# A gated MLP's down projection as two-by-two block products with seven multiplications

## The chip, the core and the metric

One core of a Trainium2 chip runs the whole program. The metric is device time in microseconds for one launch. Engines are named as in the profile: PE (TensorE matmul), PEld (its weight loads), DVE (VectorE), ACT (ScalarE), POOL (GpSimd), SP (SyncE, which issues the loads).

## The reference

Two decoder layers work on x of 256 tokens by 2048 features, in float32. Each layer adds a mixer's output to x (layer 0: gated spatial mixing and a gated linear recurrence; layer 1: attention) and then that of a gated MLP. The change is in the MLP alone:

```python
def conv_ffn(h, w_up, conv_w, conv_b, w_down):
    seq = h.shape[1]
    z = h @ w_up                                   # 2048 -> 2 x 5632
    zp = jnp.pad(z, ((0, 0), (CONV_WIDTH - 1, 0), (0, 0)))
    z = sum(conv_w[j] * zp[:, j:j + seq] for j in range(CONV_WIDTH)) + conv_b
    a, b = jnp.split(z, 2, axis=-1)
    return (jax.nn.silu(a) * b) @ w_down           # 5632 -> 2048
...
        h = rms_norm(x, ffn_norm[l])
        x = x + conv_ffn(h, ffn_w_up[l], ffn_conv_w[l], ffn_conv_b[l], ffn_w_down[l])
```

## The kernel before

**Layout.** Features lie on the 128 partitions, tokens on the free axis. x is 16 tiles xT[m] of 128 features by 256 tokens. The 5632 hidden features are 44 tiles (HT), the up projection has 88 blocks: 44 for a, 44 for b.

**Three products for one.** Every float32 matrix product is made of faster matmuls on a rounded part and its remainder. For a weight chunk w, `weights` loads it from SP's queue (L137), ACT copies it into wh with rounding (L139), and DVE computes the remainder wl = w - wh (L141). The activations were split in the same way (`split`, L200 and L201), with both parts side by side in one tile of 512 columns. `project` then runs, for each tile of 128 input features, one matmul of wh with all 512 columns (L155) and one of wl with the 256 rounded columns (L157), accumulating in one PSUM bank. This pair is the unit of work in both projections. A later operation adds the bank's two halves.

**Buffers.** The pool wp has four buffers for w and three each for wh and wl. Inside the MLP a second pool (fw, kept in `deep`) adds four w, two wh and two wl, and every other chunk goes there. PSUM has three banks pm for projections and five others for the rest, in pools that live for the whole program.

**Order inside the MLP.** The program text gives the order, and a static scheduler settles how each engine's stream interleaves; every engine then works its stream in order. The hidden tiles are worked in four groups of eleven (GRP). `up(g)` makes 22 up blocks: `conv` is a projection over 16 feature tiles in two chunks of eight (16 pairs), the addition of the halves (L187, L188), the norm's factor R (L195) and the width-3 convolution (L673 on ACT, L674 and L675 on DVE); for each a and b there follow Silu on ACT, the product (L685) and the split into a tile hid. `down(g)` projects a group's eleven hidden tiles on each of the 16 output tiles m (chunks of 6 and 5 tiles, 11 pairs) and `add_x` adds the result to xT[m]: ACT copies one half out of PSUM (L264), DVE adds the other and then the copy (L265, L266). The order is up(0), up(1), down(0), up(2), down(1), up(3), down(2), down(3). In layer 0 the last `down` also feeds the next norm: a split of xT[m] (L203, L204) and its square (L239, L240). In layer 1 it stores xT[m] instead (L696).

Of the kernel before, what the change touches and what calls it, by code (L numbers as in the profile page):

```python
# [19 lines left out]
CH = 16  # L20
HID = 5632
HT = HID // P
GRP = 11
EPS = 1e-6
WARM = 12
LEVELS = (64, 32, 16, 8, 4, 2, 1)
# [18 lines left out]
def tile_trunk(ctx: ExitStack, tc: tile.TileContext, x, pp_d, cst_d, mlev_d, msk_d,  # L45
# [8 lines left out]
    pm = ctx.enter_context(tc.tile_pool(name="pm", bufs=3, space=bass.MemoryType.PSUM))  # L54
    px = ctx.enter_context(tc.tile_pool(name="px", bufs=1, space=bass.MemoryType.PSUM))

    count = [0]

    def nm(base):
        count[0] += 1  # L60
        return f"{base}_{count[0]}"
# [36 lines left out]
    def back(ap):  # L98
        return view(ap, P - 1, (-1, P))

    def bank(tag="px"):
        n = nm(tag)
        return px.tile([P, 512], F32, tag=tag, name=n, bufs=banks[tag])

    banks = {"px": 5}
    flight, queue = [], []

    def tick():
# [11 lines left out]
    warm = pm.tile([P, 512], F32, tag="pm", name="warm")  # L120
    for i in range(WARM):
        PE.matmul(warm[:, 0:P], ones, ones, start=True, stop=True)

    def drain():
        while flight or queue:
            tick()

    deep = {"pool": None, "turn": 0}

    def weights(src, n):  # L130
        deep["turn"] += 1
        if deep["pool"] is not None and deep["turn"] > 6 and deep["turn"] % 2:
            pool, nw, ns = deep["pool"], 4, 2
        else:
            pool, nw, ns = wp, 4, 3
        w = pool.tile([P, n], F32, tag="w", name=nm("w"), bufs=nw)
        nc.sync.dma_start(w, src)  # L137
        wh = pool.tile([P, n], F32R, tag="wh", name=nm("wh"), bufs=ns)
        SC.activation(wh, w, AF.Copy)  # L139
        wl = pool.tile([P, n], F32R, tag="wl", name=nm("wl"), bufs=ns)  # L140
        V.tensor_tensor(wl, w, wh.bitcast(F32), ALU.subtract)  # L141
        return wh, wl

    def project(wsrc, acts, chunks=(8, 8), k0=0):
        ps = pm.tile([P, 512], F32, tag="pm", name=nm("pm"))
        nk = sum(chunks)
        done = 0
        for c in chunks:
            lo = (k0 + done) * P
            tick()  # L150
            wh, wl = weights(wsrc[:, lo:lo + c * P], c * P)
            for k in range(c):
                a = acts[done + k]
                first, last = done + k == 0, done + k == nk - 1
                PE.matmul(ps, wh[:, k * P:(k + 1) * P], a,  # L155
                          start=first, stop=False, skip_group_check=True)
                PE.matmul(ps[:, S:2 * S], wl[:, k * P:(k + 1) * P], a[:, 0:S],  # L157
                          start=False, stop=last, skip_group_check=True)
            done += c
        return ps  # L160

    def project_tok(wsrc, norm, feed=False):
        ps = [pm.tile([P, 512], F32, tag="pm", name=nm("pm")) for _ in range(2)]
# [58 lines left out]
    class Norm:  # L222
# [21 lines left out]
            self.feed_split(k)  # L244
            self.feed_square(k)

        def finish(self, tok=False):
            ps = bank()
# [12 lines left out]

    def add_x(m, ps):
        t = tp.tile([P, S], F32, tag="ev", name=nm("ev"), bufs=3)
        SC.activation(t, ps[:, S:2 * S], AF.Copy)  # L264
        V.tensor_tensor(xT[m], xT[m], ps[:, 0:S], ALU.add)  # L265
        V.tensor_tensor(xT[m], xT[m], t, ALU.add)  # L266

# [1 line left out]
    def mixer_ab(norm):  # L269
        es = ExitStack()  # L270
        hp = es.enter_context(tc.tile_pool(name="hp", bufs=1))

        def quad(n):
            return hp.tile([P, 512], F32R, tag="two", name=nm(n), bufs=2 * NH)
# [258 lines left out]
        es.close()  # L533
        return nxt

# [1 line left out]
    def mixer_c(norm):  # L537
        es = ExitStack()
        hp = es.enter_context(tc.tile_pool(name="cpool", bufs=1))
        dp = es.enter_context(tc.tile_pool(name="dp", bufs=1, space=bass.MemoryType.DRAM))  # L540
        A = norm.a
        R, Rt = norm.finish(tok=True)
# [109 lines left out]
        es.close()  # L652
        return nxt

# [1 line left out]
    def ffn(l, norm, last):  # L656
        es = ExitStack()
        hp = es.enter_context(tc.tile_pool(name="fp", bufs=1))
        deep.update(pool=es.enter_context(tc.tile_pool(name="fw", bufs=1)), turn=0)
        A = norm.a  # L660
        R = norm.finish()
        nxt = None if last else Norm(C_MIX + KT)

        def conv(j):
            z = project_norm(w_up[l, j], A, R)
# [12 lines left out]
        def up(g):  # L678
            hid = []
            for i in range(GRP):  # L680
                j = g * GRP + i
                a = conv(j)
                b = conv(HT + j)
                act(a, a, AF.Silu)
                V.tensor_tensor(a, a, b, ALU.mult)  # L685
                t = hp.tile([P, 512], F32R, tag="hid", name=nm("hid"), bufs=2 * GRP)
                split(t, a)
                hid.append(t)
            return hid

        def down(g, hid):
            for m in range(KT):
                add_x(m, project(w_dn[l, m], hid, chunks=(6, 5), k0=g * GRP))
                if g == HT // GRP - 1:
                    if last:
                        nc.sync.dma_start(out[:, m, :], xT[m])  # L696
                    else:
                        nxt.feed(m)

        hids = [up(0)]  # L700
        for g in range(HT // GRP):
            if g + 1 < HT // GRP:
                hids.append(up(g + 1))
            down(g, hids[g])
        deep["pool"] = None
        es.close()
        return nxt

    banks.update(px=3, pd=2)
    norm = mixer_ab(Norm(C_MIX))  # L710
    norm = ffn(0, norm, False)
    norm = mixer_c(norm)
# [81 lines left out]
```

## Time and profile before

| | |
|---|---|
| time, median of 3 runs | 2391.18 us (2377.88 to 2404.29) |
| span of the profiled execution, first to last instruction | 2389.0 us (the page gives no other time for it) |
| PE, PEld | 2377.3 us (100%), 2060.0 us (86%) |
| DVE | 1756.3 us (74%) |
| ACT | 1317.2 us (55%) |
| POOL | 16.1 us (1%) |
| DMA packets | 440.73 MB, mean 184 GB/s |

Rows of groups read: line, engine, operation, tiles, shapes and count, then the busy time in us and the mean ns of one, then the idle time just before them and what ended it. Busy time is the time covered, so overlapping instructions of a group count once. Rows of waits read: who waited for whom, us in total, times, the longest. Rows of stretches read: start and end, length, then busy us and instructions of each engine, the granted clock, the share of the DMA engines' time and GB/s.

### The profile page before, as it was taken

What the parts mean: (1) busy time and instruction counts of PE and PEld (TensorE: products, weight loads), DVE (VectorE), ACT (ScalarE), POOL (GpSimd) and SP (SyncE); (2) the same over time, 40 slices, a digit from 0 to 9 for tenths busy, and PEclk for the clock granted to TensorE, in tenths of its full rate; (3) what the DMA queues carried; (4) which work ended last, traced back from release to release, by engine and by line L of the source; (5) the groups of instructions that cost most, each with busy time, mean ns of one, the idle gap of its engine ahead of it and who ended that gap; (6) DMA issues with size and microseconds to landing.
All of it is one profiled execution on the core that took longest, in us unless ns stands there. A gap on an engine that the chain in (4) does not pass through costs nothing.

```text
span 2389.0 us, 35728 instructions
## 1 busy us (share of the span) xinstructions
PE 2377.3 (100%) x13198; PEld 2060.0 (86%) x13198; DVE 1756.3 (74%) x2954; ACT 1317.2 (55%) x2169; POOL 16.1 (1%) x20
## 2 busy tenths in 40 slices
PE   8999999999999999999999999999999999999999
PEld 7888888888888888888888888888888888888888
DVE  6767786888867877777756666777777767767765
ACT  6655565655555555555545455556555555545543
POOL 2000000000000000000000000000000000000000
PEclk9999999999999999999999999999999999999999
DMA  7544455755566566566655555557555565565564
GB/s 265 177 159 135 141 184 187 241 190 191 169 187 213 177 173 222 176 170 188 200 175 177 175 159 167 188 192 237 186 186 186 156 220 186 152 220 185 153 188 145
DMA packets 133869, 440.73 MB, mean 184 GB/s; under 512 B 14880, under 2 KB 16944, under 8 KB 133440
## 3 DMA queue, kind: packets, MB, share of 16 engines
q1 hardware_dynamic: 132224, 433.40, 57.5%
q10 hardware_dynamic: 1440, 5.01, 0.6%
q8 instruction: 104, 1.70, 0.3%
q14 instruction: 69, 0.57, 0.1%
q0 software_dynamic: 32, 0.05, 0.0%
HBM read 436.29 MB, written 2.11 MB: 184 GB/s over the span
## 4 chain that ended last, share of the span: by engine, by line
PE 97%; DMA 1%; DVE 1%; issue 0%; ACT 0%; SPq 0%; DVEq 0%; ACTq 0%
PE pm L155 53%; PE pm L157 27%; PE pm L177 5%; PE pm L178 5%; PE pm L176 5%; PE px L439 1%; DVE wl L141 0%; DMA w<-in_w_v 0%; DMA mst<-in_mlev 0%; PE pd L411 0%; DMA w<-in_w_up 0%; PE pd L412 0%; PE px L612 0%; PE px L576 0%; PE px L583 0%
## 5 line engine op out<-in xcount | busy, mean ns | idle before, releaser
L141 DVE TENSOR_TENSOR wl<-w,wh 128x1024 fp32r<-128x1024 f32 (+3 forms) x900 | 1015.7, 1129 | 538.1 <-ACT wh L139 534.3
L139 ACT ACTIVATE wh<-w 128x1024 fp32r<-128x1024 f32 (+3 forms) x900 | 883.4, 982 | 952.2 <-PE pm L155 653.4
L155 PE MATMUL pm<-a,wh 128*128 128x512 f32 x3600 | 1266.0, 396 | 0.0
L157 PE MATMUL pm<-a,wl 128*128 128x256 f32 x3600 | 1010.5, 281 | 0.5 <-DVE wl L141 0.5
L155 PEld LDWEIGHTS pm<-a,wh 128*128 128x128 f32 x3600 | 675.0, 187 | 157.1 <-DVE a L204 0.8
L157 PEld LDWEIGHTS pm<-a,wl 128*128 128x128 f32 x3600 | 680.3, 189 | 1.6 <-DVE wl L141 0.8
L155 PE MATMUL pm<-hid,wh 128*128 128x512 f32 x1408 | 493.1, 395 | 0.0
L157 PE MATMUL pm<-hid,wl 128*128 128x256 f32 x1408 | 394.8, 280 | 0.0
L155 PEld LDWEIGHTS pm<-hid,wh 128*128 128x128 f32 x1408 | 263.9, 187 | 61.9
L157 PEld LDWEIGHTS pm<-hid,wl 128*128 128x128 f32 x1408 | 266.0, 189 | 0.0
L176 PE MATMUL pm<-wh,a 128*128 128x512 f32 x512 | 204.0, 400 | 2.1 <-ACT wh L139 2.1
L177 PE MATMUL pm<-wl,a 128*128 128x512 f32 x512 | 202.0, 395 | 3.5 <-DVE wl L141 3.5
L178 PE MATMUL pm<-wh,a 128*128 128x512 f32 x512 | 201.6, 394 | 0.0
L177 PEld LDWEIGHTS pm<-wl,a 128*128 128x128 f32 x512 | 97.0, 189 | 25.3 <-DVE wl L141 5.9
L176 PEld LDWEIGHTS pm<-wh,a 128*128 128x128 f32 x512 | 97.2, 190 | 21.7 <-ACT wh L139 2.4
L178 PEld LDWEIGHTS pm<-wh,a 128*128 128x128 f32 x512 | 96.7, 189 | 20.2
L673 ACT ACTIVATE conv<-ev,pp 128x256 f32<-128x256 f32 x176 | 103.4, 587 | 16.2 <-DVE ev L195 16.2
L188 DVE TENSOR_TENSOR ev<-pm,ev 128x256 f32<-128x256 f32 x225 | 93.8, 417 | 3.4 <-ACT ev L187 3.4
L674 DVE SCALAR_TENSOR_TENSOR conv<-ev,pp,conv 128x255 f32<-128x255 f32 x176 | 84.2, 478 | 8.1 <-ACT conv L673 8.1
L675 DVE SCALAR_TENSOR_TENSOR conv<-ev,pp,conv 128x254 f32<-128x254 f32 x176 | 85.1, 483 | 6.2
L155 PE MATMUL pm<-yc,wh 128*128 128x512 f32 x256 | 88.8, 391 | 0.0
L195 DVE TENSOR_TENSOR ev<-ev,R 128x256 f32<-128x256 f32 x184 | 78.3, 425 | 6.1
(181 smaller groups left out, 1602.7 us busy)
## 6 DMA issues: line engine op xcount, KB each, us to landing
w<-in_w_up SPq DMA_DIRECT2D x352, 512.0 KB, 4.3
w<-in_w_dn SPq DMA_DIRECT2D x128, 384.0 KB, 3.2
w<-in_w_cqkv SPq DMA_DIRECT2D x96, 512.0 KB, 3.6
w<-in_w_dn SPq DMA_DIRECT2D x128, 320.0 KB, 3.3
w<-in_w_abo SPq DMA_DIRECT2D x32, 512.0 KB, 4.3
w<-in_w_cg SPq DMA_DIRECT2D x32, 512.0 KB, 3.9
w<-in_w_co SPq DMA_DIRECT2D x32, 512.0 KB, 3.5
w<-in_w_f SPq DMA_DIRECT2D x16, 512.0 KB, 3.6
```

The costliest lines, as they stand in the source:

```text
L139: SC.activation(wh, w, AF.Copy)
L141: V.tensor_tensor(wl, w, wh.bitcast(F32), ALU.subtract)
L155: PE.matmul(ps, wh[:, k * P:(k + 1) * P], a, start=first, stop=False, skip_group_check=True)
L157: PE.matmul(ps[:, S:2 * S], wl[:, k * P:(k + 1) * P], a[:, 0:S], start=False, stop=last, skip_group_check=True)
L176: PE.matmul(ps[T], ah, h, start=k + i == 0, stop=False)
L177: PE.matmul(ps[T], ah, l, start=False, stop=False)
L178: PE.matmul(ps[T], al, h, start=False, stop=k + i == KT - 1)
L188: V.tensor_tensor(t, ps[:, 0:S], t, ALU.add)
L195: V.tensor_tensor(out, t, R, ALU.mult)
L673: SC.activation(c, z, AF.Identity, bias=pp[:, cb:cb + 1], scale=w(2))
L674: V.scalar_tensor_tensor(c[:, 1:], z[:, :S - 1], w(1), c[:, 1:], ALU.mult, ALU.add)
L675: V.scalar_tensor_tensor(c[:, 2:], z[:, :S - 2], w(0), c[:, 2:], ALU.mult, ALU.add)
```

## The change

Only the MLP computes in another way. The sums of its down projection are taken in two-by-two blocks: two hidden tiles (a pair) by two token halves on one side, two hidden tiles by two halves of the outputs on the other. Block products of such matrices can be had from seven multiplications in place of eight, with sums of blocks before and after.

- The 44 hidden tiles are 22 pairs. The first 20 go through block products, in groups of three pairs (the last of two); the last two pairs (TAIL) are projected as before, in 32 chunks of four tiles.
- `ups` is a generator of up blocks. Twelve run first (LEAD), then two for each step. For each pair, DVE combines the gated products into eight blocks u of 128 tokens, and ACT and DVE split seven of them into the tile S (14 blocks of 128 columns).
- `step` works one pair against one half of the outputs (un: output tiles 8 un to 8 un + 7). It loads X, 2 hidden tiles by 8 output tiles, in pieces of 1 KB. DVE makes the sums T1, T2 (t12) and T3, T4 (t34), 512 columns each. Seven products follow, each three matmuls of 512 weight columns with the split S block as the stationary side, so tokens are now on the partitions of the result. They fill seven PSUM banks (qa, qb, qc, qd); the eighth is pm, for the up blocks.
- `evacuate` adds the seven banks into acc after each group (a copy on ACT the first time), and after the last group combines the seven sums into the four result blocks.
- At the end, each output tile m takes its block from acc by two transposes on PE and an addition to xT[m]; then come the projection of the last two pairs and `add_x`.
- Some remainders are made without DVE: ACT writes -w, rounded, into a tile wd, and a transfer from POOL's queue adds w to it in place. This holds for the second chunk of two out of three up blocks after the first twelve, and for the half X[:, 1024:2048] of each step.
- The pool fw goes; the up blocks' PSUM is copied whole by ACT (tile e, 512 columns) and its halves are added from there. PSUM pools are opened for each stage.

```diff
-GRP = 11
+PAIRS = HT // 2
+GROUPS = (3, 3, 3, 3, 3, 3, 2)
+TAIL = PAIRS - sum(GROUPS)
+LEAD = 12
...
+    def halves(w, n, how):
+        if how is not None:
+            wl = how.tile([P, n], F32R, tag="wd", name=nm("wd"), bufs=3)
+            SC.activation(wl, w, AF.Copy, scale=-1.0)
+            nc.gpsimd.dma_start(wl, w, accum_op=ALU.add)
+        wh = wp.tile([P, n], F32R, tag="wh", name=nm("wh"), bufs=3)
+        SC.activation(wh, w, AF.Copy)
+        if how is None:
+            wl = wp.tile([P, n], F32R, tag="wl", name=nm("wl"), bufs=3)
+            V.tensor_tensor(wl, w, wh.bitcast(F32), ALU.subtract)
+        return wh, wl
...
     def ffn(l, norm, last):
-        deep.update(pool=es.enter_context(tc.tile_pool(name="fw", bufs=1)), turn=0)
+        banks_of(es, qa=1, qb=1, qc=1, qd=1, pm=1)
...
+        def ups():
...
+                    for jj in (j, HT + j):
+                        early = n < LEAD
+                        ab.append(conv(jj, "qb" if early and n % 2 else "pm",
+                                       None if early or n % 3 == 0 else hp))
...
+                        V.tensor_tensor(view(u, (1 if i else 3) * P, (-P, 2), (1, P)), a3, b3, ALU.mult)
+                    if i and not plain:
+                        V.tensor_tensor(u[:, 4:6], u[:, 0:1].to_broadcast([P, 2, P]), u[:, 1:3], ALU.subtract)
+                        V.tensor_tensor(u[:, 6], u[:, 1], u[:, 5], ALU.subtract)
+                        V.tensor_tensor(u[:, 7], u[:, 3], u[:, 6], ALU.subtract)
+                        us = u[:, 1:8].rearrange("p a b -> p (a b)")
+                        SC.activation(t[:, 0:7 * P], us, AF.Copy)
+                        V.tensor_tensor(t[:, 7 * P:14 * P], us, t[:, 0:7 * P].bitcast(F32), ALU.subtract)
...
+        def step(g, un, i, k0, first, lastp, q):
+            x = hp.tile([P, 2048], F32, tag="X", name=nm("X"), bufs=2)
+            nc.sync.dma_start(x.rearrange("p (m c) -> p m c", m=8),
+                              w_dn[l, 8 * un:8 * un + 8, :, k * P:(k + 2) * P].rearrange("m p c -> p m c"))
...
+            V.tensor_tensor(t12, view(x, 0, (0, 2), (2 * P, 4), (1, P)),
+                            view(x, P, (7 * P, 2), (2 * P, 4), (1, P)), ALU.add)
+            V.tensor_tensor(t34[:, 0], t12[:, 0], b12, ALU.add)
+            V.tensor_tensor(t34[:, 1], t34[:, 0], b22, ALU.add)
+            def product(slot, sidx, wh, wl):
+                sh, sl = (t[:, (o + sidx) * P:(o + sidx + 1) * P] for o in (0, 7))
+                PE.matmul(q[slot], sh, wh, start=first, stop=False)
+                PE.matmul(q[slot], sh, wl, start=False, stop=False)
+                PE.matmul(q[slot], sl, wh, start=False, stop=lastp)
+            wh, wl = halves(t34.rearrange("p a b c -> p (a b c)"), 1024, None)
+            product(0, 5, wh[:, 0:512], wl[:, 0:512])
+            product(1, 3, wh[:, 512:1024], wl[:, 512:1024])
...
+            product(2, 4, h21, l21)
+            next(feed, None)
+            wh, wl = halves(t12.rearrange("p a b c -> p (a b c)"), 1024, None)
+            product(3, 1, wh[:, 0:512], wl[:, 0:512])
+            product(4, 6, wh[:, 512:1024], wl[:, 512:1024])
+            wh, wl = halves(x[:, 1024:2048], 1024, hp)
+            for slot, sidx, o in ((5, 0, P), (6, 2, 0)):
+                product(slot, sidx, *(view(v, o, (2 * P, 4), (1, P)) for v in (wh, wl)))
...
+        for g, n in enumerate(GROUPS):
+            for un in range(2):
+                qt = [(bank("qa", 2), 2), (bank("qb"), 1), (bank("qc", 2), 2), (bank("qd", 2), 2)]
...
+                for i in range(n):
+                    next(feed, None)
+                    step(g, un, i, k0, i == 0, i == n - 1, q)
+                evacuate(g, un, qt)
...
+        for m in range(KT):
+            tps = bank(("qa", "qc", "qd")[m % 3], 2)
+            for T in range(2):
+                PE.transpose(tps[:, T * P:(T + 1) * P], d[:, c[T], (m % 4) * P:(m % 4 + 1) * P], ident)
+            V.tensor_tensor(xT[m], xT[m], tps[:, 0:S], ALU.add)
+            add_x(m, project(w_dn[l, m], ks, chunks=(2 * TAIL,), k0=2 * k0, tag=("pm", "qb")[m % 2]))
```

More of the change, by code (lines that the diff above doesn't have):

```diff
@@ L119, in tile_trunk, with warmup @@
         (SC if i else nc.sync).dma_start(t, x[:, c0:c0 + n, :])
-    warm = pm.tile([P, 512], F32, tag="pm", name="warm")
-    for i in range(WARM):
-        PE.matmul(warm[:, 0:P], ones, ones, start=True, stop=True)
+    def warmup():
+        warm = bank("pm")
+        for i in range(WARM):
+            PE.matmul(warm[:, 0:P], ones, ones, start=True, stop=True)
     def drain():
@@ L126, in drain, with weights, project @@
             tick()
[L128 to L136, printed above, removed]
-        nc.sync.dma_start(w, src)
[L138 to L145, printed above, removed]
+    def halves(w, n, how):
[9 more added lines that the diff above has]
+        return wh, wl
+    def weights(src, n, how=None):
+        w = wp.tile([P, n], F32, tag="w", name=nm("w"), bufs=4)
+        nc.sync.dma_start(w, src)
+        return halves(w, n, how)
+    def project(wsrc, acts, chunks=(8, 8), k0=0, tag="pm", how=None):
+        ps = bank(tag)
         nk = sum(chunks)
@@ L150, in project @@
             tick()
-            wh, wl = weights(wsrc[:, lo:lo + c * P], c * P)
+            wh, wl = weights(wsrc[:, lo:lo + c * P], c * P, how if done else None)
             for k in range(c):
@@ L162, in project_tok @@
     def project_tok(wsrc, norm, feed=False):
-        ps = [pm.tile([P, 512], F32, tag="pm", name=nm("pm")) for _ in range(2)]
+        ps = [bank("pm") for _ in range(2)]
         k = 0
@@ L676, in conv @@
             return c
[L678 to L696, printed above, removed]
-                    else:
-                        nxt.feed(m)
@@ new lines, in evacuate, with two @@
+        def evacuate(g, un, qt):
+            o = 0
+            for t, n in qt:
+                d = acc[un][:, o:o + n].rearrange("p a b -> p (a b)")
+                if g == 0:
+                    SC.activation(d, t, AF.Copy)
+                else:
+                    V.tensor_tensor(d, d, t, ALU.add)
+                o += n
+            if g == len(GROUPS) - 1:
+                d = acc[un]
+                Q1, Q6, Q4, Q2, Q7, Q3, Q5 = range(7)
+                def two(i, j):
+                    return view(d[:, i], 0, ((j - i) * 512, 2), (1, 512))
+                V.tensor_tensor(two(Q7, Q6), two(Q7, Q6), two(Q1, Q1), ALU.add)
+                V.tensor_tensor(two(Q7, Q6), two(Q7, Q6), two(Q4, Q3), ALU.add)
+                V.tensor_tensor(two(Q7, Q6), two(Q7, Q6), two(Q5, Q2), ALU.subtract)
+                V.tensor_tensor(two(Q4, Q3), two(Q4, Q3), two(Q2, Q5), ALU.add)
@@ new lines, in ffn @@
+        ks = [t[:, i * 512:(i + 1) * 512] for t in pairs[k0:] for i in range(2)]
+        for m in range(KT):
+            d = acc[m // 8]
+            c = (4, 2) if m % 8 < 4 else (5, 1)
+            tps = bank(("qa", "qc", "qd")[m % 3], 2)
[3 more added lines that the diff above has]
+            add_x(m, project(w_dn[l, m], ks, chunks=(2 * TAIL,), k0=2 * k0, tag=("pm", "qb")[m % 2]))
+            if last:
+                nc.sync.dma_start(out[:, m, :], xT[m])
+            else:
+                nxt.feed(m)
@@ L706, in ffn @@
         es.close()
         return nxt
-    banks.update(px=3, pd=2)
     norm = mixer_ab(Norm(C_MIX))
```

77 lines of the change are left out of this document (60 added, 17 removed).

## The prediction

> **What bounds the kernel now.** I read the first part of the page (busy time by engine), then the chain that ended last, then stretches of the trace.
>
> ```profile
> span 2389.0 us, 35728 instructions
> PE 2377.3 (100%) x13198; PEld 2060.0 (86%) x13198; DVE 1756.3 (74%) x2954; ACT 1317.2 (55%) x2169; POOL 16.1 (1%) x20
> PE 97%; DMA 1%; DVE 1%; issue 0%; ACT 0%; SPq 0%; DVEq 0%; ACTq 0%
> ```
>
> The matmuls are the kernel: 97% of the chain is PE, so a matmul removed is time removed, as long as the others keep up. Next, three stretches (us; then busy time and instructions of PE, PEld, DVE, ACT, POOL; clock; DMA share; GB/s): the MLP of layer 0, that of layer 1, and a piece of the attention's input projection, where PE runs only 128x512 matmuls.
>
> ```profile
> 423.00:1161.50 738.50, 738.50 (x4259) 650.66 (x4257) 570.89 (x916) 417.77 (x673) 0.00 (x0) 1.00 0.61 190
> 1637.00:2389.00 752.00, 747.33 (x4228) 647.39 (x4226) 555.82 (x880) 401.06 (x636) 0.00 (x0) 1.00 0.59 184
> 1180.00:1225.00 45.00, 45.00 (x201) 37.24 (x200) 28.95 (x37) 20.83 (x25) 0.00 (x0) 1.00 0.67 216
> ```
>
> The MLPs hold 738.5 + 752.0 = 1490.5 us. There DVE works 1126.7 us (76%), ACT 818.8 us (55%), PE all the time. The waits of layer 0's MLP say how much slack the feeding engines have:
>
> ```profile
> ACT wh L139 <- PE pm L155: 273.6, 253, 1.7
> DVE wl L141 <- ACT wh L139: 150.7, 271, 1.7
> ```
>
> ACT waits for PE to free a buffer, and DVE waits for ACT: both are ahead of PE, and PE has no wait worth a row.
>
> **What PE saves.** In the grouped matmuls of layer 0's MLP one wh and one wl matmul form a pair; the busy time of the wh group covers the pair.
>
> ```profile
> L155 PE MATMUL pm<-hid,wh 128*128 128x512 f32 x704 | 244.2, 391 | 0.0
> L576 PE MATMUL px<-cst,z 128*128 128x128 f32 x64 | 8.3, 272 | 0.0
> ```
>
> 704 pairs in 244.2 us is 0.347 us a pair. Two layers lose 2 x 640 pairs: -444.2 us. They gain 2 x 40 steps x 7 products x 3 matmuls = 1680 matmuls of 512 columns, at 45.00/201 = 0.2239 us each: +376.1 us. The 64 transposes of the end match the 64 of L576: +8.3 us. Net -59.8 us. With PE alone as bound the MLPs would take 1430.7 us.
>
> **What DVE and ACT get.** Unit prices are the mean ns of these groups (layer 0's MLP; 128x512, 128x128 and the 577 ns PSUM read from the whole run).
>
> ```profile
> L141 DVE TENSOR_TENSOR wl<-w,wh 128x1024 fp32r<-128x1024 f32 x178 | 217.9, 1225 | 87.8 <-ACT wh L139 87.4
> L141 DVE TENSOR_TENSOR wl<-w,wh 128x768 fp32r<-128x768 f32 x64 | 61.3, 958 | 31.8 <-ACT wh L139 31.6
> L141 DVE TENSOR_TENSOR wl<-w,wh 128x640 fp32r<-128x640 f32 x64 | 52.7, 824 | 31.7 <-ACT wh L139 31.7
> L266 DVE TENSOR_TENSOR x<-x,ev 128x256 f32<-128x256 f32 x65 | 27.6, 425 | 2.2
> L265 DVE TENSOR_TENSOR x<-x,pm 128x256 f32<-128x256 f32 x65 | 26.9, 414 | 0.0
> L201 DVE TENSOR_TENSOR hid<-conv,hid 128x256 fp32r<-128x256 f32 x44 | 18.4, 418 | 1.4 <-ACT hid L200 1.4
> L204 DVE SCALAR_TENSOR_TENSOR a<-x,pp,a 128x256 fp32r<-128x256 f32 x17 | 8.2, 481 | 1.2 <-ACT a L203 1.2
> L240 DVE TENSOR_TENSOR acc<-acc,sq 128x256 f32<-128x256 f32 x17 | 7.1, 419 | 0.0
> L219 DVE TENSOR_TENSOR junk<-z 128x512 f32<-128x512 f32 x16 | 11.0, 686 | 0.8
> L451 DVE TENSOR_TENSOR st<-st,smk 128x128 f32<-128x128 f32 x56 | 17.1, 305 | 1.4
> L139 ACT ACTIVATE wh<-w 128x1024 fp32r<-128x1024 f32 x178 | 188.8, 1062 | 196.0 <-PE pm L155 190.3 <-issue 3.9 <-DMA w<-in_w_up 1.5
> L139 ACT ACTIVATE wh<-w 128x768 fp32r<-128x768 f32 x64 | 54.1, 845 | 59.1 <-PE pm L155 42.3 <-issue 16.8
> L139 ACT ACTIVATE wh<-w 128x640 fp32r<-128x640 f32 x64 | 47.3, 739 | 42.5 <-PE pm L155 41.0
> L187 ACT ACTIVATE ev<-pm 128x256 f32<-128x256 f32 x88 | 32.2, 366 | 0.0
> L200 ACT ACTIVATE hid<-conv 128x256 fp32r<-128x256 f32 x44 | 18.0, 409 | 8.8 <-DVE conv L685 8.8
> L89 ACT ACTIVATE pd<-pd 128x512 f32<-128x512 f32 x32 | 17.6, 577 | 0.8 <-ACT pd L89 0.6
> ```
>
> DVE loses, over both layers: 100 remainders of up blocks, now made by adding transfers (122.5 us), the down remainders (128 x 0.958 + 128 x 0.824 = 228.1), 96 of 128 residual updates (96 x 0.839 = 80.5), 80 products and splits of the hidden (80 x 0.843 = 67.4): 498.5 us. It gains: 160 remainders of block sums (196.0), 80 sums T1, T2 (98.0), 160 of T3, T4 (109.8), 80 remainders of B21 (54.9), the hidden's products and combinations (80 x 0.425 + 40 x (0.425 + 2 x 0.305 + about 1.09 for 896 columns) = 119.0), 24 evacuations into acc (24 x (3 x 1.225 + 0.686) = 104.7), 16 last combinations (19.6), the end's 32 remainders and 32 transpose adds (35.2): 737.2 us. Net +238.7, so 1126.7 becomes 1365 us: 95% of 1430.7.
>
> ACT gains 180 negated copies and 240 copies of 1024 columns (446.0), 80 of 512 (0.63 each, from the 640 row: 50.6), 0.211 more on each of 176 evacuations (37.1), 40 splits of 896 (about 0.95: 38.0), first evacuations and the end's copies (35.0); it loses 202.8 + 32.7 + 35.1 us of down copies, hidden copies and residual evacuations. Net +336, so 81%.
>
> So the change buys 60 us of the bound engine with 239 us on DVE and 336 us on ACT, in stretches where these have 364 and 672 us free. All of it must be hidden under PE. Two places where it is not:
>
> *The end of each layer.* The last two steps run without up blocks, then come two evacuations, the combinations and the plain remainder. DVE: 2 x 5.74 (one step: 1.225 + 2 x 0.686 + 1.225 + 0.686 + 1.225) + 2 x 4.36 + 8 x 1.225 + 16 x (0.686 + 0.414 + 0.414 + 0.425) = 61.0 us, and in layer 0 16 x 0.900 more for the next norm (L204, L240). PE in the same place: 42 x 0.2239 + 64 x 0.347 + 4.2 = 35.8 us. PE waits 25 + 40 = 65 us over both layers if nothing was done ahead. DVE at 95% can hardly be ahead, and the three wl buffers limit it; I take 55, bounds 15 and 75.
>
> *The rounds.* A round is two up blocks and a step: PE 32 x 0.347 + 21 x 0.2239 = 15.8 us; 38 rounds a layer. The MLP loses its extra pool (four w, two wh, two wl), so wh and wl have three buffers each, for eight wh chunks a round. After the three products on T3, T4 and B21 (9 x 0.2239 = 2.02 us) an up chunk needs the wh buffer that was freed just before them: ACT 1.06 and then DVE 1.23 us make 2.29 us even if both were idle, and 0.22 us of cover comes from the first wh matmul. At 81% and 95% they are seldom idle: half an operation on DVE and some of one on ACT, 0.6 to 0.9 us, come on top. pm has one bank now, so the same 2.02 us must also hold ACT's 0.58 us evacuation, and behind an ACT evacuation that waits for PE, or a convolution that waits for DVE, stands the next wh for everyone. PE is in order too: one late wl holds all products and up blocks behind it. I take 0.9 us a round, 76 x 0.9 = 68 us. Bounds: 0 (the static order hides it) and 2.3 us (a whole turn-around open: 175 us).
>
> Stage borders: each stage now has its own PSUM pool, so a border can wait for the last evacuation; I take 0, bound one evacuation each (2 us in all).
>
> **The transfers.** 180 adding transfers of 0.524 MB go through POOL's queue, which held one load before. The step's X load takes 1 KB pieces.
>
> ```profile
> q1 hardware_dynamic: 132224, 433.40, 57.5%
> pp<-in_pp POOLq DMA_DIRECT2D x1, 50.0 KB, 6.3
> q1 hardware_dynamic: 576, 0.52, 11.9%
> ```
>
> The first row gives 0.575 x 2389.0 / 433.40 = 3.17 us per MB. The last is that queue in the final 13 us (2376 to 2389), where only 1 KB pieces of out move: 0.119 x 13 / 0.52 = 2.98 us per MB, so small pieces cost nothing. Per round: four w and one X, 3.15 MB, 9.97 us; 7/3 adding transfers, 1.22 MB, 3.88 us if they cost as a load: 13.9 of 15.8 us, hidden. No row shows an adding transfer. Below, its cost is a load's; from above I use twice that, since an add reads its destination as well, 17.7 us a round, not hidden. I take the lower for the sum, since 3.17 contains queueing, and keep the upper as a rival. [...] A w buffer is free only once its adding transfer has landed, and SP's queue is in order, so the next w and X loads queue behind that wait; with the 6.3 us of the POOL row this fits into four w and two X buffers.
>
> **The sum.** 2389.0 - 59.8 + 55 + 68 = 2452 us. The page gives the profiled execution no time besides its span; the median is 2391.18, so I add 2: 2454 us (2.6% slower). DVE would be busy 1365 of 1554 us, 88%. That is between the MLP's 76% and the highest stretches of the trace:
>
> ```profile
> 260.00:280.00 20.00, 20.00 (x129) 17.97 (x128) 17.21 (x48) 10.18 (x22) 0.00 (x0) 1.00 0.40 132
> 320.00:340.00 20.00, 19.91 (x115) 17.21 (x114) 18.44 (x38) 15.73 (x33) 0.00 (x0) 1.00 0.58 188
> ```
>
> **Rivals.** *Faster:* PE stays the bound. For it: DVE at 86% left PE whole, and at 92% PE lost only 0.09 us of 20; and DVE instructions that don't wait for each other overlap (start, length):
>
> ```profile
> 908.95 1.23 DVE L141 TENSOR_TENSOR wl<-w,wh 128x1024 fp32r<-128x1024 f32 x1 [0.51 <-ACT wh L139]
> 910.10 0.41 DVE L265 TENSOR_TENSOR x<-x,pm 128x256 f32<-128x256 f32 x1
> ```
>
> The second starts 0.08 us before the first ends, so 95% may be some points less. Against: those stretches are 20 us long, the MLPs 1430. With no stall in the rounds and 20 us at the ends: 2389 - 60 + 20 + 2 = 2351. *No change:* DVE at 1365/1490.5 = 91.6% throughout; gain and loss cancel, 2391. It decides between the forecast and the faster case: 0.07 us of stall a round. *Slower by transfers:* an adding transfer costs over 1.5 loads (5.84 us a round left for 3.88); then queues, not DVE, set the round. At two loads: 76 x (17.7 - 15.8) = 144, so 2389 - 60 + 55 + 144 + 2 = 2530. For it: the DMA share is 0.61 already, and the latency of POOL's queue; against:
>
> ```profile
> 5.00:10.00 5.00, 2.90 (x13) 2.09 (x12) 2.31 (x9) 2.43 (x6) 0.00 (x0) 1.00 1.03 398
> ```
>
> at 398 GB/s the round's loads take 7.9 us, and an adding transfer could cost 2.6 loads.
>
> **Chances and range.** Forecast 0.45 (its own range 2415 to 2520), faster 0.26, no change 0.14, transfers 0.15. So faster by over 1% 0.26, within 1% 0.14, slower 0.60; 1%, 24 us, is about what a measurement of this kernel tells from no change (its runs lie 2377.88 to 2404.29). The range leaves out the best of the faster case (2331) and the worst of transfers and rounds: 2340 to 2600.
>
> **What would show it.** Right: PE 60 us less busy work by count but with waits on wl and wh in the MLPs; DVE 85 to 92% there; a stretch of some 60 to 75 us at each MLP's end with PE half idle. Wrong: DVE over 92% with PE whole (faster); PE's waits on wd, or SP's queue waiting for adding transfers with the DMA share near 1 (transfers); products dearer than 0.2239 us.

## The result and the profile after

The changed kernel takes 2724.01 us (median of 4 runs, 2721.42 to 2726.64), the one before 2390.91 us: a ratio of 1.137, 95% interval 1.132 to 1.143. The forecast was 2454 us, its range ended at 2600. The sign was right and the size was not: 273 us of the profiled span (2724.8 against the 2452 of the sum) have to be found.

Two parts of the page after the change: busy times, then the chain that ended last, by engine and by line.

```profile
span 2724.8 us, 34419 instructions
PE 2475.6 (91%) x12382; PEld 2052.1 (75%) x12382; DVE 1933.9 (71%) x3142; ACT 1617.1 (59%) x2325; POOL 169.3 (6%) x200
PE 57%; DVE 15%; DMA 13%; ACT 9%; issue 6%; ACTq 0%; SPq 0%; DVEq 0%; POOLq 0%
PE pm L162 24%; PE pm L164 13%; DMA w<-in_w_up 12%; DVE wl L143 6%; ACT wh L140 5%; PE pm L184 4%; PE pm L185 4%; PE pm L183 4%; DVE acc L784 2%; PE qb L162 2%; ACT e L676 1%; ACT wd L137 1%; PE qb L164 1%; ACT S L727 1%; DVE ev L678 1%
```

PE held 97% of the chain before and holds 57% now. New in it are DVE (15%, 1% before), ACT (9%, before 0%) and a load, w from the up projection's weights (12%). PE has fewer matmuls and yet more busy time (2377.3 us before), so some run slower: the 128x512 ones from a and wh take 417 ns in mean, before 396.

Stretches after the change (columns as before). In each layer: the first twelve up blocks and one more, up to the first product; the rounds, up to the last up block; the end.

```profile
424.10:502.30 78.20, 75.54 (x420) 65.49 (x420) 62.13 (x100) 48.29 (x67) 2.48 (x3) 0.98 0.63 203
502.30:1262.50 760.20, 661.26 (x3189) 538.56 (x3189) 528.00 (x780) 478.58 (x604) 73.20 (x87) 0.94 0.78 215
1262.50:1331.70 69.20, 50.69 (x214) 36.73 (x212) 62.83 (x118) 36.97 (x74) 0.85 (x1) 0.85 0.32 92
1819.80:1896.70 76.90, 74.23 (x419) 65.32 (x419) 61.90 (x100) 48.31 (x67) 2.07 (x3) 0.98 0.64 206
1896.70:2662.00 765.30, 666.58 (x3190) 543.71 (x3189) 528.15 (x780) 477.97 (x603) 73.59 (x87) 0.93 0.78 213
2662.00:2720.30 58.30, 46.06 (x214) 35.17 (x212) 52.85 (x93) 24.16 (x43) 0.84 (x1) 0.88 0.39 113
```

The rounds are where the time went. With the prediction's prices a stretch of them holds 75 up blocks (75 x 16 x 0.347 us) and 38 steps (38 x 21 x 0.2239 us), 595.1 us of PE, and with 0.9 us of stall for each step 629.3 us. They took 760.2 and 765.3: 267 of the 273 us. PE idles 98.9 and 98.7 us in them, at a mean clock of 0.94 and 0.93. DVE is 69% busy there, where the prediction had 88% for the whole MLP: it isn't the bound, it waits as well.

Waits of the whole run after the change (who waited for whom: us in total, times, longest):

```profile
DVE wl L143 <- ACT wh L140: 557.5, 372, 6.1
ACT wh L140 <- PE pm L162: 319.0, 211, 6.1
ACT wd L137 <- DMA w<-in_w_up: 187.3, 52, 6.4
PE pm L162 <- ACT e L676: 94.7, 24, 5.5
PE pm L162 <- ACT wh L140: 39.5, 14, 4.0
PE pm L164 <- DVE wl L143: 39.4, 78, 1.5
```

Read from below: PE waits for ACT and DVE, and DVE for ACT. ACT waits for two things: 52 times for a load, 3.6 us each, and 211 times for PE, which has to free a wh buffer first. The largest of PE's rows is 24 stops of 3.9 us before e. One of them, in the chain of layer 0 (start, us, what) and in stretches of 2 us, some left out:

```profile
935.14 0.95 ACT wh L140
936.09 0.02 issue
936.11 8.57 DMA w<-in_w_up
944.68 0.02 issue
```
```profile
944.77 1.06 ACT L137 ACTIVATE wd<-w 128x1024 fp32r<-128x1024 f32 x1 [5.85 <-DMA w<-in_w_up]
948.14 0.79 PE L162 MATMUL pm<-a,wh 128*128 128x512 f32 x1 [4.95 <-ACT e L676]
```
```profile
932.00:934.00 2.00, 2.00 (x12) 1.66 (x11) 0.26 (x1) 1.35 (x2) 0.00 (x0) 1.00 1.12 158
940.00:942.00 2.00, 2.00 (x12) 1.68 (x11) 1.68 (x4) 0.00 (x0) 0.00 (x0) 1.00 1.05 272
944.00:946.00 2.00, 0.00 (x0) 0.00 (x0) 0.00 (x0) 1.23 (x2) 0.00 (x0) 0.86 0.03 12
946.00:948.00 2.00, 0.00 (x0) 0.00 (x0) 1.20 (x2) 2.00 (x4) 0.85 (x1) 0.50 0.33 63
948.00:950.00 2.00, 1.86 (x5) 1.59 (x6) 2.00 (x4) 1.99 (x3) 0.00 (x0) 0.50 1.12 199
```

ACT finishes with a w buffer at 936.09, and only then the next load starts. It takes 8.57 us beside other transfers: from 934 to 944 the DMA share lies between 0.78 and 1.28. ACT stands before the chunk, to make its wd, for 5.85 us. Behind it, in ACT's order, stand the copy out of PSUM (e) that PE waits for, and the wh copies of two chunks that had landed at 930.28 and 931.54. PE idles 4.95 us. Meanwhile the DMA engines run dry (0.03 at 944 to 946), because no buffer is free to load into: the next load waits for the buffer of the first of these two chunks, which DVE is done with at 948.03, and starts at 948.06. When PE returns its clock is 0.50, and a pair of its matmuls takes 0.64 us (948.95 to 951.51, four pairs), against 0.35 from 952.90 to 954.29. It was 0.50 without a gap of this length too: in e1 (below) no gap of PE in the rounds is longer than 2.2 us, and yet its clock is 0.50 for 55 us of them.

The transfers, by queue (packets, MB, share of the span of 16 engines), and by issue (KB each, median us to landing):

```profile
q1 hardware_dynamic: 183168, 433.39, 48.2%
q0 software_dynamic: 25952, 94.43, 18.7%
w<-in_w_up SPq DMA_DIRECT2D x352, 512.0 KB, 4.4
wd<-w POOLq DMA_DIRECT2D x100, 512.0 KB, 5.7
wd<-X POOLq DMA_DIRECT2D x80, 512.0 KB, 7.1
```

An MB of adding transfers costs 0.187 x 2724.8 / 94.43 = 5.40 us of the 16 engines, an MB of loads 0.482 x 2724.8 / 433.39 = 3.03 us: 1.78 loads, above the 1.5 at which the prediction's rival was to decide.

### The profile page after: what moved, and what is told of

It reads as the page before. It is cut to its first block, busy times and chain, and to the rows that moved or that the text cites. A ratio compares the mean times of both kernels' runs of the same rounds, so it can differ in the third digit from the quotient of the medians.

```text
span 2724.8 us, 34419 instructions
## 1 busy us (share of the span) xinstructions
PE 2475.6 (91%) x12382; PEld 2052.1 (75%) x12382; DVE 1933.9 (71%) x3142; ACT 1617.1 (59%) x2325; POOL 169.3 (6%) x200
## 3 DMA queue, kind: packets, MB, share of 16 engines
q1 hardware_dynamic: 183168, 433.39, 48.2%
q0 software_dynamic: 25952, 94.43, 18.7%
## 4 chain that ended last, share of the span: by engine, by line
PE 57%; DVE 15%; DMA 13%; ACT 9%; issue 6%; ACTq 0%; SPq 0%; DVEq 0%; POOLq 0%
PE pm L162 24%; PE pm L164 13%; DMA w<-in_w_up 12%; DVE wl L143 6%; ACT wh L140 5%; PE pm L184 4%; PE pm L185 4%; PE pm L183 4%; DVE acc L784 2%; PE qb L162 2%; ACT e L676 1%; ACT wd L137 1%; PE qb L164 1%; ACT S L727 1%; DVE ev L678 1%
## 5 line engine op out<-in xcount | busy, mean ns | idle before, releaser
L143 DVE TENSOR_TENSOR wl<-w,wh 128x1024 fp32r<-128x1024 f32 (+1 forms) x576 | 686.5, 1192 | 548.4 <-ACT wh L140 546.5
L140 ACT ACTIVATE wh<-w 128x1024 fp32r<-128x1024 f32 (+1 forms) x676 | 694.5, 1033 | 559.4 <-PE pm L162 220.8
L164 PE MATMUL pm<-a,wl 128*128 128x256 f32 x2608 | 779.2, 299 | 36.0 <-DVE wl L143 35.0
L164 PEld LDWEIGHTS pm<-a,wl 128*128 128x128 f32 x2608 | 530.4, 203 | 74.0 <-DVE wl L143 70.8
L164 PE MATMUL pm<-a,wd 128*128 128x256 f32 x800 | 224.9, 281 | 0.0
L137 ACT ACTIVATE wd<-w 128x1024 fp32r<-128x1024 f32 x100 | 105.4, 1054 | 187.4 <-DMA w<-in_w_up 187.3
L138 POOL DMA_DIRECT2D wd<-w x100 | 85.0, 850 | 2063.0 <-DMA w<-in_w_up 1088.4
L143 DVE TENSOR_TENSOR wl<-T,wh 128x1024 fp32r<-128x1024 f32 x160 | 195.5, 1222 | 11.0 <-ACT wh L140 11.0
L140 ACT ACTIVATE wh<-T 128x1024 fp32r<-128x1024 f32 x160 | 167.5, 1047 | 3.2 <-DVE T L752 1.1
L164 PEld LDWEIGHTS pm<-a,wd 128*128 128x128 f32 x800 | 152.2, 190 | 0.0
```

The costliest lines, as they stand in the source:

```text
L137: SC.activation(wl, w, AF.Copy, scale=-1.0)
L138: nc.gpsimd.dma_start(wl, w, accum_op=ALU.add)
```

## The experiments

Sixteen kernels, each a small edit of the changed kernel. "Rounds" is the sum of both layers' stretches of rounds; the changed kernel has 1525.5 us there. Ratios are to the kernel before in the same job. e2, e3 and e12 to e14 do the whole computation; the others leave the addition of w out or mix sums in one place, and keep the rest of the work.

| kernel | us | ratio (95%) | rounds |
|---|---|---|---|
| e1_noadd | 2578.06 | 1.078 (1.075 to 1.081) | 1381 |
| e2_dveall | 2545.95 | 1.065 (1.060 to 1.069) | 1334 |
| e3_pool | 2652.73 | 1.109 (1.106 to 1.113) | 1447 |
| e4_plaincopy | 2656.34 | 1.111 (1.102 to 1.120) | 1467 |
| e5_w7 | 2452.26 | 1.024 (1.015 to 1.032) | 1260 |
| e6_noadd_w7 | 2449.62 | 1.022 (1.014 to 1.031) | 1260 |
| e7_noadd_wh5 | 2416.00 | 1.006 (1.004 to 1.008) | 1222 |
| e8_noadd_pm2 | 2577.97 | 1.076 (1.066 to 1.086) | 1373 |
| e9_shared | 2719.15 | 1.139 (1.131 to 1.147) | 1524 |
| e10_wh5 | 2517.25 | 1.055 (1.047 to 1.062) | 1315 |
| e11_w5 | 2500.83 | 1.048 (1.041 to 1.054) | 1312 |
| e12_fold_w7 | 2617.36 | 1.095 (1.090 to 1.099) | 1429 |
| e13_wd2_w5 | 2614.02 | 1.091 (1.083 to 1.098) | 1420 |
| e14_dveall_w7 | 2536.92 | 1.060 (1.053 to 1.066) | 1334 |
| e15_mix | 2432.01 | 1.016 (1.007 to 1.024) | 1237 |
| e16_fold_shared | 2618.76 | 1.098 (1.091 to 1.106) | 1429 |

### Who makes the remainders

Four kernels change the adding transfers alone.

```diff
 e1_noadd
-            nc.gpsimd.dma_start(wl, w, accum_op=ALU.add)
 e2_dveall
     def halves(w, n, how):
+        how = None
 e3_pool: after wh, in place of the negated copy and the transfer
+            nc.gpsimd.tensor_tensor(wl, w, wh.bitcast(F32), ALU.subtract)
 e4_plaincopy
-            nc.gpsimd.dma_start(wl, w, accum_op=ALU.add)
+            nc.gpsimd.dma_start(wl.bitcast(F32), w)
```

**e1_noadd.** 

> The 180 adding transfers are left out: ACT still writes -w into wd and PE uses that, so the remainders are wrong, and ACT, DVE, PE and the loads keep all their work. Theory L (late loads: an adding transfer takes the DMA engines twice a load's time, holds its w buffer, and the next w arrives late for ACT, whose order puts wd ahead of the copies that everyone needs): most of the 333 us goes, 2400 to 2500 us, ACT's waits of wd for w (187 us) fall below 40, DMA share in the rounds from 0.78 to about 0.6. Rival T (turn-around: three wh and wl buffers and one pm bank, as forecast): 2600 us or more, PE's waits on e and wh stay.

**e2_dveall.** 

> All remainders on DVE, no adding transfer and no wd: ACT loses 190 us, DVE gains 180 x 1.225 = 220 us. Theory L: DVE becomes the bound of the rounds, 1365 + 220 = 1585 us of single durations in MLPs of 1490 before: 2440 to 2560 us, no waits for w. Rival T: DVE is fuller and the three buffers as before, so slower than the changed kernel: 2750 us or more.

**e3_pool.** 

> The 180 remainders as subtractions on GpSimd from w and wh, in place of -w on ACT and the adding transfer. One took 1.02 us for 256 columns, so about 4.1 us for 1024, 740 us in all, half of POOL's time in the MLPs. Theory L: 2400 to 2500 us, as without the transfers, and ACT lighter by 190 us. Rival T: the remainder now comes after wh and 4 us later, so no better than the changed kernel: 2700 us or more.

**e4_plaincopy.** 

> The 180 transfers copy w into wd without adding (the remainder is wrong): same bytes, same queue, same waits and holds, one read fewer. If the price of the addition matters (5.4 us per MB of added data in the trace against 3.03 for loads), the time falls by about half of what e1 gains, to 2560 or so. If the hold of w and the latency through POOL's queue matter, it stays above 2660. Rival T: 2720.

Without any transfer 146 us go (2724.01 - 2578.06) and 187 of the 333 us of loss stay, so the transfers are a part of the cause and not all of it. e1 lies between the bands of the two theories and bears out neither; ACT still waits 90.1 us for loads, where under 40 was expected. e2 lies in the first theory's band. A copy in the add's place (e4) gives back 68 of the 146, about the half that was expected; the 2560 given beside it doesn't follow from that half. The queue of POOL in e4 and the first of e3's groups on POOL:

```profile
q0 software_dynamic: 25952, 94.43, 9.0%
L142 POOL TENSOR_TENSOR wd<-w,wh 128x1024 fp32r<-128x1024 f32 x100 | 247.8, 2478 | 1695.3 <-ACT wh L136 1216.9 <-DVE wl L139 472.8 <-issue 5.6
```

A copy costs 0.09 x 2664.0 / 94.43 = 2.54 us per MB, so the add (5.40) costs 2.1 times a copy.

e3 (2653) missed both bands, and it is 107 us worse than DVE alone (e2). GpSimd's subtraction takes 2.48 us, not the 4.1 expected, where DVE's takes 1.2, and PE waits for it only 14 us in all. But it holds DVE up. DVE's multiplication by R in the changed kernel, then in e3:

```profile
L679 DVE TENSOR_TENSOR ev<-ev,R 128x256 f32<-128x256 f32 x176 | 74.3, 422 | 3.4
L678 DVE TENSOR_TENSOR ev<-ev,R 128x256 f32<-128x256 f32 x176 | 243.2, 1382 | 3.4
```

In e3 it takes 0.42 us in the 77 cases in which no subtraction of GpSimd runs beside it, and 2.13 us in mean in the 99 in which one does. That this makes the 107 us is likely and not shown. So e3 says little about the transfers.

### How deep the buffers are

The next kernels add buffers in the MLP. Their room comes from one accumulator for both halves of the output blocks, in which the sums mix.

```diff
+    def chunk(tag, n, dt, bufs):     # in place of wp.tile for w, wh and wl
+        if turn["pool"] is not None and more.get(tag):
+            turn[tag] = turn.get(tag, -1) + 1
+            if turn[tag] % (bufs + more[tag]) >= bufs:
+                return turn["pool"].tile([P, n], dt, tag=tag + "2", ..., bufs=more[tag])
+        return wp.tile([P, n], dt, tag=tag, name=nm(tag), bufs=bufs)
...
-        acc = [hp.tile([P, 7, 512], F32, tag="acc", ..., bufs=2) for _ in range(2)]
+        acc = [hp.tile([P, 7, 512], F32, tag="acc", ..., bufs=1)] * 2
 e5 more = w: 3   e6 the same, without the transfers   e7 wh: 2, wl: 1, without the transfers
 e9 none (the control)   e10 wh: 2, wl: 1   e11 w: 1   e15 w: 1, wh: 1, wl: 1
 e8, without the transfers and with two accumulators:
-        banks_of(es, qa=1, qb=1, qc=1, qd=1, pm=1)
+        banks_of(es, qa=1, qc=1, qd=1, pm=2)
```

**e5_w7.** 

> The changed kernel with seven w buffers in place of four in the gated MLP (the room comes from one accumulator that both halves of the output blocks share, so that the sums in it are wrong; the work is the same). Theory L (loads start late, because a buffer comes free late, and ScalarE, which works in order, stands before the chunk that is not there): the 187 us in which ScalarE waits for a load fall under 60, the rounds go from 20.0 us to about 18.2, which is what they take without the adding transfers, and the time from 2724 to about 2590. Theory B (the 16 DMA engines have no slack: 3 MB of loads at 3.03 us and 1.17 MB of adding transfers at 5.40 us are 15.4 us of each round, and more buffers make no engine faster): 2700 to 2725.

**e6_noadd_w7.** 

> The same seven w buffers, without the adding transfers (the remainder that they make is wrong). Theory L: the 90 us in which ScalarE still waits for loads without them go too, 2578 becomes about 2500. Theory T (what is left is turn-around between TensorE, ScalarE and VectorE): no change, 2565 to 2580.

**e7_noadd_wh5.** 

> Without the adding transfers, with five wh and four wl buffers in place of three each (room from the shared accumulator; remainder and sums are wrong). Theory T in its form with the halves' buffers (ScalarE's wh waits until TensorE lets a wh buffer go, and VectorE's wl behind it): 2578 becomes about 2500, the rounds go from 18.2 to about 17.2 us. Theory L, or the bank: 2565 to 2580.

**e8_noadd_pm2.** 

> Without the adding transfers, and with a second bank for the up blocks (the third product is added into the bank of the first, so its sum is wrong; the work of each engine is the same but for the smaller stage end). Theory T in its form with the bank (an up block's first product waits until ScalarE has read the bank of the block before): the 20 us of such waits go, and the clock that is lost behind them; 2578 becomes 2530 to 2555. The other theories: 2570 to 2580.

**e9_shared.** 

> The control for the two kernels with more buffers: the changed kernel with the one shared accumulator and nothing else (the sums in it are wrong, the work is the same). Theory D (the depth of the buffers is the cause): 2715 to 2730, as the changed kernel. Rival (the shared accumulator itself, smaller and elsewhere in memory, made the time): about 2452, and then the seven buffers did nothing.

**e10_wh5.** 

> The changed kernel, adding transfers and all, with five wh and four wl buffers in place of three each and four w buffers as it has (room from the shared accumulator). Theory D in its wide form (any three more buffers in the chain load, halves, product let the loads run ahead): 2430 to 2480, as with seven w buffers. Rival, the narrow form (an adding transfer holds its w buffer for 6 to 7 us more, so with transfers only more w buffers help): 2560 to 2650, the rounds 18 us or more.

**e11_w5.** 

> The changed kernel with five w buffers in place of four (shared accumulator). If each buffer is worth the same, a third of the 272 us that three brought: about 2630. If one is enough, as where a load was late by a fixed few us only: 2460 to 2500. If the transfers need all three: over 2690.

**e15_mix.** 

> The changed kernel with five w, four wh and four wl buffers (shared accumulator, sums in it wrong). If both places limit together: the rounds go to 16.2 us, the time to about 2420. If w alone is what the transfers need: 2470 to 2500, as with five w buffers alone. Seven w buffers gave 2452; the halves alone 2517.

The shared accumulator itself makes 5 us (e9). Three more w buffers give back 267 us against this control (2719.15 - 2452.26), nearly the whole miss, and one gives 218 of them (e11, at the edge of "one is enough"). Theory B's band (2700 to 2725) is clearly missed, and theory L's 2590 was too timid by 138 us. The stretches of rounds of e5, then its wait for loads, PE's waits for wl and e, two queues and the up loads:

```profile
500.00:1129.60 629.60, 618.91 (x3190) 511.21 (x3189) 526.13 (x780) 476.97 (x604) 72.99 (x86) 1.00 0.94 257
1759.90:2390.20 630.30, 619.25 (x3190) 511.24 (x3189) 526.01 (x780) 476.52 (x604) 73.00 (x86) 1.00 0.94 257
```
```profile
ACT wh L150 <- DMA w<-in_w_up: 29.3, 15, 2.2
PE pm L174 <- DVE wl L153: 16.4, 35, 2.6
PE pm L172 <- ACT e L687: 4.1, 12, 0.3
```
```profile
q1 hardware_dynamic: 183168, 433.39, 53.7%
q0 software_dynamic: 25952, 94.43, 20.7%
w<-in_w_up SPq DMA_DIRECT2D x352, 512.0 KB, 5.3
```

The same instructions on every engine take 130.6 us less in layer 0. PE's idle time falls from 98.9 to 10.7 us; the other 42.4 us are PE's own busy time (661.26 to 618.91 for the same matmuls). Most of that is the clock: in the changed kernel PE was busy for 76 us of this stretch at 0.50, which costs 38 us; in e5 it is 1.00 throughout. The prices per MB are as before (0.537 x 2450.5 / 433.39 = 3.04 us; 5.37 for the adds), and the DMA share rises to 0.94 with ScalarE waiting 29 us for loads in place of 187: with seven buffers the transfers stream, with four they come in bursts with empty stretches between. The transfers then cost nothing that can be seen: e6, without them, is 2449.62, some 50 us below the lower of the two theories.

e7 shows that w need not be the place. With two more wh and one more wl the chain load, halves, product also runs ahead, and without transfers this is the best of all (2416, where the theory had 2500). With the transfers it is worth 202 us (e10, between what the two theories gave). One of each (e15) comes to 2432, near the 2420 given for both places limiting together. The bank is not the place, as far as it was tried, without transfers: e8 equals e1. The rounds of layer 0 in e7, then in e15:

```profile
501.90:1113.10 611.20, 607.52 (x3189) 514.31 (x3188) 520.18 (x779) 479.95 (x603) 0.00 (x0) 1.00 0.58 193
```
```profile
500.80:1119.80 619.00, 608.85 (x3189) 513.39 (x3188) 522.74 (x779) 475.89 (x603) 73.16 (x86) 1.00 0.95 263
```

In both PE is left within 4 and 10 us of whole. The DMA share tells what the transfers take, 0.95 x 619.0 against 0.58 x 611.2, 234 of 588 us, nearly all of it hidden.

### Room from inside the kernel

Four kernels keep two accumulators, or fold.

```diff
 e12_fold_w7: four sums in place of seven, 12 adds of 512 in evacuate(), w: 3
-        acc = [hp.tile([P, 7, 512], F32, ...
+        acc = [hp.tile([P, 4, 512], F32, ...
+            put(O6, q6); put(O7, q1); more(O6, q1); put(O4, q4); more(O7, q4); ...
 e16_fold_shared: the same with one accumulator of four sums
 e13_wd2_w5: w: 1, and
-            wl = how.tile([P, n], F32R, tag="wd", name=nm("wd"), bufs=3)
+            wl = how.tile([P, n], F32R, tag="wd", name=nm("wd"), bufs=2)
 e14_dveall_w7: e2's edit, and w: 3 in the room of wd
```

**e12_fold_w7.** 

> The whole computation, with seven w buffers whose room is won honestly: the seven products of a group are folded into four sums of 512 when they leave the banks (12 adds of 512 in place of 7 per group and half, and no combining at the end), so that the accumulators take 8 KB in place of 14. Theory D (depth alone made the loss, and 2452 is what is left): 2452 plus what the folding costs; 28 evacuations times 5 adds of about 0.6 us is 84 us of VectorE, which is 0.84 busy in the rounds, so most of it is hidden: 2460 to 2500, the rounds 16.7 to 17.4 us. Rival (what keeps the time above 2391 lies in the accumulators or the turn-around at a group's end, which the folding makes longer): over 2520.

**e13_wd2_w5.** 

> The whole computation: five w buffers and two wd buffers in place of four and three, separate accumulators, combined at the end as in the changed kernel. Theory D (depth in w, and the folding alone spoiled the run with the folded sums): 2500 (the five buffers with the shared accumulator) to 2560, a few tens of us lost to the missing wd buffer. Rival (depth does nothing where the accumulators are apart, or three wd buffers are what the transfers need): 2650 or more.

**e14_dveall_w7.** 

> The whole computation: no adding transfers, every remainder on VectorE, and the 12 KB of the wd buffers given to w (seven). VectorE then has 0.92 to 0.93 of the 17.6 us of a round, 16.3 us, more than TensorE's 15.8, and must be the bound. Theory D: the rounds fall to 16.8 to 17.2 us, 2546 becomes 2480 to 2515. Rival (where VectorE is the bound, buffers before it give nothing): 2530 to 2550.

**e16_fold_shared.** 

> Seven w buffers and the folding at each group's end, with one accumulator of four sums that both halves share (the sums in it are wrong, the work is that of the folded kernel). If the folding cost the 165 us (five more adds for VectorE at 28 group ends, 80 us, and the clock behind the gaps): 2605 to 2625. If the accumulators being apart cost them: about 2455 to 2480.

The folding came out in the rival's band, 165 us above e5, and e16, which folds into a shared accumulator, took the same: the folding is the cost, not the separate accumulators. The rounds of layer 0 and the row of e12's waits that grew (e5: 16.4):

```profile
501.10:1216.20 715.10, 644.93 (x3189) 534.70 (x3188) 568.52 (x877) 477.16 (x604) 73.15 (x86) 0.95 0.83 227
```
```profile
PE pm L174 <- DVE wl L153: 122.8, 50, 5.7
```

DVE got 568.52 - 526.13 = 42 us more in layer 0, as expected, but 85.5 us were lost there: 59.5 in PE's idle time (70.2 against 10.7 us), 26.0 in its busy time, at a mean clock of 0.95. The expectation read DVE's mean of 0.84 as cover. The adds come in one block at each group's end, and no wl is made meanwhile: up to 10.1 us pass there between two of them, in e5 at most 4.4.

e13 missed both bands (2614). The fifth w buffer helps here as well, by 110 us against the changed kernel, but the third wd buffer was needed: e11, which has it (and the shared accumulator), is 113 us faster. This row is new:

```profile
PE pm L174 <- DMA wd<-w: 81.5, 26, 5.3
```

e14 gives 9 us for three buffers, as its rival said. Its rounds of layer 0, beside e2's:

```profile
501.30:1169.30 668.00, 627.14 (x3189) 518.34 (x3188) 617.77 (x866) 408.63 (x518) 0.00 (x0) 0.98 0.51 174
```
```profile
501.10:1170.80 669.70, 627.38 (x3189) 518.69 (x3188) 617.74 (x866) 408.58 (x518) 0.00 (x0) 0.98 0.52 175
```

With DVE at 0.92 (617.77 / 668.00) loads no longer matter, and DVE is the likely bound, some 8% above its own sum; more wh or wl buffers were not tried with it. No kernel here with the whole computation beats the one before; the nearest is e14.

## Why the prediction was right or wrong

- *What PE saves* (-59.8 us): too much by some 25 us. Where PE hardly waits (e7), it is busy 607.5 and 607.2 us in the stretches of rounds, by the prediction's prices 595.1.
- *The end of each layer* (+55): right in the sum, in part by luck. 69.2 + 58.3 us less twice 35.8 of PE make 55.9. But PE idles only 30.8 us in them (18.5 and 12.2); 25 us are busy time beyond the prices, at a clock of 0.85 and 0.88, which the working didn't have.
- *The work of DVE and ACT* (+238.7, +336): right as a sum of single durations, which rises by 223.9 and 325.2 us. The busy time rises by less, since instructions that overlap count once in it: the six stretches after hold 1295.9 us of DVE, 169 more than before, and 1114.3 of ACT, 295 more. It did not matter: DVE waited.
- *The rounds* (0.9 us a step, 68 us, bounds 0 and 175): wrong for the kernel as it is, which loses 335 us there against PE's prices. The working counted turn-arounds between PE, ACT and DVE with the data always there. e5's rounds, 629.6 and 630.3 us against 629.3, agree by luck: PE idles 11 us in each where the term had 34, and is busy 24 us above the prices.
- *The transfers*: this step failed, in its last sentence. A w buffer was to come free once its adding transfer has landed, and "with the 6.3 us of the POOL row this fits into four w and two X buffers". That put late loads at nothing, and no sum was made. A round of 15.8 us uses four chunks, so with four buffers each may be held 15.8 us on average. In the trace of the changed kernel, followed chunk by chunk through the rounds of layer 0 (loads, copies and remainders matched in the order of the program), they are held for 20.2. And it isn't the transfer that holds them. For the 50 chunks that have one it lands 13.2 us after the load's issue, but the chunk's wh copy ends only 19.0 us after it: in ACT's order wd comes early, and wh, which needs a buffer that PE frees, ends 12.8 us after wd has begun. The transfer was the last user of 3 of the 50 buffers. Chunks without a transfer hold theirs longer still, 20.8 us, of which they lie 13.2 landed and not yet copied. The largest row of SP's queue, which issues the loads in order, and its row of the transfers say the same:

```profile
SPq L148 <- DVE wl L143: 970.7, 280, 30.3
SPq L148 <- DMA wd<-w: 39.4, 26, 4.4
```

- *Why more buffers help, in w or in wh* (an estimate from the same traces): a chunk with a transfer needs its load, 5.5 us in mean, and the 12.8 us from wd to the end of wh. That makes 18.3 and doesn't fit into 15.8. Seven w buffers have room for 27.7 (in e5 the two are 5.0 and 16.2). Five wh and four wl buffers shorten the second to 10.2 (e7, without transfers, with a load of 4.9); with transfers it is 10.7 beside a load of 5.9 (e10), a little too long again. Without transfers and with no buffer more (e1) such a load takes 4.2 us: the sum is 16.4, still too long, and 123 of the 267 us stay in the rounds. So the transfers make the loads later, and too few buffers make late loads count. No run changed the other part, ACT's order of wd before wh.
- *The price of an adding transfer*: the sum took a load's price, the rival two, both estimates without a row; it is 1.78 (5.40 against 3.03 us per MB). The rival "Slower by transfers" had the sign and a time (2530) nearer to the result, but not the mechanism: it made throughput the limit, and e5 carries all transfers at 2452.
- *No change* (DVE the bound at 91.6%): not what happened, DVE is at 69% in the rounds. e2 and e14 suggest that such a bound exists where DVE does everything.
- *Stage borders* (0, bound 2) and the first up blocks: by the prices 72.2 us of PE in 78.2 and 76.9, so 11 us in all that the sum didn't have.

So what too few buffers cost, put at nothing, is 267 of the 273 us; e5 against its control e9 shows it. About two thirds of it is waiting and a third PE's longer busy time behind the waits (88.2 and 42.4 us in layer 0). That e5 comes out at 2452 beside a forecast of 2454 is chance: its other errors nearly cancel.

## What to carry to other kernels

When a change adds a step to a buffer's life, add up the time from the load's issue to the last reader's end, in the order in which the engines work, and hold it against buffers times the time between uses. Here that was 18.3 us against 15.8, an estimate from the trace. The step that was added need not be the last reader: here the transfer landed 13.2 us after the load's issue, and the copy behind it ended 19.0 us after it. Buffers that were too few showed here as an in-order engine standing before a load (ACT, 187.3 us in 52 waits; with three more w buffers 29.3), with the DMA engines idle for a part of it (a share of 0.03 from 944 to 946). A block of work on a feeding engine was not hidden by that engine's mean idle time (e12: DVE at 0.84 in e5's rounds, and 42 us more of it cost 85.5 us in layer 0). That remainders made ahead would hide it is an estimate; no run shows it.

## What was not expected of the hardware

- The half clock (0.50 for 76 us of PE's busy time in the rounds of layer 0, 1.00 throughout in e5): in the rounds of the changed kernel the same matmuls take 42.4 us (layer 0) and 47.3 us (layer 1) more of busy time than in e5; each 1 us of idling cost about half a us more (42.4 us for 88.2 in layer 0).
- An adding transfer within SBUF costs 5.40 us per MB of the 16 engines, a plain one on the same queue 2.54, a load 3.03.
- At a DMA share of 0.94, held for 630 us, an up load takes 5.3 us to land (median) where it took 4.4 at 0.78, and yet ACT waits for such loads 29.3 us in place of 187.3, with seven w buffers in place of four (e5).
- While a subtraction of GpSimd runs, DVE's multiplication by R takes 2.13 us in mean in place of 0.42 (e3).
